# Sparse-attention block: queries with features on the partitions, stacked per head through DRAM

## The chip, the cores and the metric

One core of a Trainium2 chip runs the whole program: two layers of a hybrid block on 528 tokens (16 meta tokens and 512 of the sequence), all in f32. The metric is device time in microseconds, the median of three runs. The engines are TensorE (PE, with PEld for its weight loads), VectorE (DVE), ScalarE (ACT), GpSimd (POOL) and SyncE (SP), which here only issues DMAs.

## The reference

Each layer normalizes its input `h` (528 x 1024) and multiplies it by `w_in`. The columns are cut into attention queries, one key and one value head, a gate, the pooled branch with its gate, index queries and keys, and the merge gates. What matters here:

```
q = apply_rope(rms_norm(q.reshape(B, T, 8, 64), qn_g), cos_h, sin_h)
k = apply_rope(rms_norm(k, kn_g), cos, sin)
q_idx = apply_rope(q_idx.reshape(B, T, 8, 64), cos_h, sin_h)
k_idx = apply_rope(k_idx, cos, sin)
# per block of 128 queries
s = einsum('bqhd,bkd->bqhk', q_idx, k_idx)
score = einsum('bqhk,bqh->bqk', relu(s), w_idx * idx_scale)   # masked by chunk
_, sel = top_k(score, 128)
p = softmax(einsum('bqhd,bqkd->bqhk', q, k[sel]) * 0.125)     # valid ones
out = einsum('bqhk,bqkd->bqhd', p, v[sel])
```

`apply_rope` takes the 64 features of a head as two halves of 32 and returns `x * cos + (-second, first) * sin`. The attention output, gated, goes through `w_a`; the pooled branch (moving means over 2, 4, 8, 16 tokens, minus the input, times `pool_w`, gated) through `w_b`; both are weighed by sigmoid gates, summed and multiplied by `w_out`, and added to the input.

## The kernel before

The normalized input stands in SBUF with features on the partitions, split into `hhi` and `hlo` (the number rounded to f32r, and the rest), so that a product is three f32r products: `hhi` and `hlo` with a weight's high part, `hhi` with its low part. Weights come in chunks of 256 columns (1 MB, in two halves on SP's queue; four `raw` buffers, so two chunks) and are split in the same way into `w` tiles, eight of them, one chunk ahead of use. Three ways of splitting exist: ACT casts the high part and DVE subtracts (`high`, `low`, L185 and L189); for the chunks in `by_dma`, ACT writes minus the weight, rounded, and a POOL DMA adds the weight onto it (`minus`, L199), then ACT casts the high part; and a mixed one for the gates.

PE and DVE run in the order in which the program is written; the scheduler orders ACT, POOL and SP. `group_done` (L331) marks the end of a group of matmuls. It runs what `later(fn, n)` put off by `n` groups, one step of weight preparation, and steps of `fill` (score products or attention, `rate` of them a group). It then lets the selection (`sel`, the 16 rounds of max and replace on DVE) advance by a credit: the priced PE time less the priced DVE time since the last group.

A query group is `tok_group` (L481): 24 matmuls with 128 tokens of `hhi` or `hlo` as the stationary operand and 256 weight columns (four heads) moving, so that queries come out with tokens on the partitions. `q_post` (L585) then makes the rope with two DVE products and a POOL sum, splits into high and low (ACT, DVE), puts both side by side in `qs`, and four PE transposes a group turn that into 128 rows (64 high, 64 low features) by head by token; ACT evicts them to `qi` or `qq`. For the normed queries it also takes squares, sums and `rsqrt` (by POOL's `pow`) into `RQ`, used as a scale in the softmax; the gain sits in the tables `Cg` and `Sg`, which POOL makes (`tables`, L434). The 16 meta tokens are a group of their own in layer 0.

The order within a layer is: keys and values of the first half, index queries of the first half (group g=0), keys and values of the second half, index queries (second half, then all four blocks of g=1); the pool gate (`silb`, two chunks); the pooled product (two chunks of `u`, POOL's running sums `us`, DVE's `finish`, PE's `mix`); `queries(0)`; the attention gate (`sila`); `queries(1)`; then `w_b` and the merge gates (`mix_gates`), with attention as `fill`, and `w_a`, `w_out`. Scores of a block are made `FI` = 6 groups after its index queries (`index_steps`, L627). `attention` calls `ensure(i)` ahead of block `i`: it runs what is left of the selection that the block needs, all at once.

Of the kernel before, what the change touches and what calls it, by code (L numbers as in the profile page):

```python
# [29 lines left out]
PB = 4  # L30
R_ATT = (1.95, 1.7)
# [7 lines left out]
FI = 6  # L39
# [3 lines left out]
QI = 3  # L43
# [45 lines left out]
def tile_block(ctx: ExitStack, tc: tile.TileContext, x, meta, w_in, pool_w, w_a, w_b, w_out, rows, hgain, c_tab, out):  # L89
# [23 lines left out]
    mixed, by_dma, plain = set(), set(), set()  # L113
    for l in range(2):
        wi = w_rows(w_in[l], 0, w_in.shape[2])

        chunks.append([(wi[:, :, 2176:2432], 0)])
# [3 lines left out]
        order = [2432, 1664, 1920, 1408, 1152, 0, 640, 896, 256]  # L121
        chunks += [[(wi[:, :, c:c + 256], 0)] for c in order]
        chunks += [[(w_rows(w_b[l], c, 512), 0)] for c in (0, 512)]
        by_dma |= set(range(len(chunks) - 10, len(chunks)))
# [38 lines left out]
    def w_prep_enqueue(casts_first=False, after=None):  # L163
# [14 lines left out]
        def split(which):  # L178
            t = w_tile().rearrange("p (k e) -> p k e", e=cols)
            parts[which].extend(t[:, k] for k in range(kt // 2))  # L180
            return t

        his = {}

        def high(s):  # L185
            his[s] = split(0)
            act.copy(his[s], raws[c][s])

        def low(s):  # L189
            dve.tensor_sub(split(1), raws[c][s], f(his[s]))  # L190
            if s == 1:
                del raws[c]
                w_load()
# [194 lines left out]
    gains = one.tile([128, 2, 2, 64], F32, name="gains")  # L388
# [3 lines left out]
    dma(gains, bass.AP(tensor=hgain.tensor, offset=hgain.offset, ap=[[0, 128], [128, 2], [64, 2], [1, 64]]))  # L392
# [27 lines left out]
    Cg = one.tile([128, 5, 64], F32, name="Cg")  # L420
    Sg = one.tile([128, 5, 64], F32, name="Sg")
    BV = one.tile([128, 4, 2, 64], F32, name="BV")
    RQ = one.tile([128, 4, NH], F32, name="RQ")
    NR = one.tile([128, 4, NH], F32, name="NR")
# [4 lines left out]
    def sheet(n, name):  # L429
        if n > HB:  # L430
            return tmp.tile([128, 544], F32, tag="L", name=name, bufs=LB)
        return tmp.tile([128, HB], F32, tag="tt", name=name, bufs=6)

    def tables(l, keys):  # L434
        if keys:
            gk = tmp.tile([128, 64], F32, tag="gk", name="gk", bufs=1)
            gp.tensor_scalar(gk, gains[:, 1, l], -0.125, None, op0=OP.mult)
        g = gk if keys else gains[:, 0, l]

        def bc(g):  # L440
            return g[:, None, :].to_broadcast([128, 5, 64])

        def sw(g):
            return g.rearrange("p (a d) -> p a d", a=2)[:, None, ::-1, :].to_broadcast([128, 5, 2, 32])

        s4 = stab.rearrange("p t (a d) -> p t a d", a=2)
        gp.tensor_tensor(Cg, ctab, bc(g), op=OP.mult)
        gp.tensor_tensor(Sg.rearrange("p t (a d) -> p t a d", a=2), s4, sw(g), op=OP.mult)
# [32 lines left out]
    def tok_group(t, w):  # L481
        e = 256
        s, m = TOK[t]
        ps = bank("d")
        for h in H:
            for k in range(KT):
                pe.matmul(ps[:m, :e], h[:, k, s:s + m], w[0][k][:, :e], start=k == 0 and h is hhi, stop=False)
                if h is hlo and k == 3:
                    half_done()
        for k in range(KT):  # L490
            pe.matmul(ps[:m, :e], hhi[:, k, s:s + m], w[1][k][:, :e], start=False, stop=k == KT - 1)
        return ps

# [23 lines left out]
    def dense(w, mt_, a, n, rhs=H, kt=KT, late=False):  # L517
        ps = bank("d")
        c = slice(mt_ * 128, (mt_ + 1) * 128)
# [4 lines left out]
        for e, (ww, r, k) in enumerate(steps):  # L524
            pe.matmul(ps[:, :n], ww[k][:, c], r[:, k, a:a + n], start=e == 0, stop=e == len(steps) - 1)
# [4 lines left out]
    def swapped(ap, h):  # L530
        return ap.rearrange("p (h a d) -> p h a d", h=h, a=2)[:, :, ::-1, :]

    def kv_post(l, t, ps):
        s, m = TOK[t]
        p2 = ps[:m, :256].rearrange("p (g c) -> p g c", g=2)[:, :, 0:64]
        sq = tmp.tile([128, 64], F32, tag="tt", name="sq", bufs=6)
# [4 lines left out]
        t1 = tmp.tile([128, HB], F32, tag="tt", name="t1", bufs=6)  # L541
        t2 = tmp.tile([128, HB], F32, tag="tt", name="t2", bufs=6)
# [475 lines left out]
    for l in range(2):  # L1018
# [152 lines left out]
        def attend():  # L1171
# [8 lines left out]
            if l == 0:  # L1180
                yield from meta_attn(qm)
# [190 lines left out]
```

## Time and profile before

| | |
|---|---|
| runs | 760.87, 763.03, 762.77 us; median 762.77 |
| profiled execution | 762.81 us, its span 761.0 us |
| granted TensorE clock | 1.0 throughout |
| busy | PE 747.4, DVE 555.5, ACT 471.4, POOL 213.6 us |
| DMA | 96.94 MB, mean 127 GB/s |

The span is the time from the first to the last instruction of the profiled execution; all shares are of it. Busy times overlap between engines, and PE's are modelled ends of pipelined matmuls, so that PE's real pace is read from where the next one starts. L numbers are lines of the kernel; every PE and DVE instruction goes through one recording helper and has its line, L61, so one goes by tile names: `d<-w,hhi` is a query group with tokens stationary, `d<-hhi,w` one with the weights stationary.

### The profile page before, as it was taken

What the parts mean: (1) busy time and instruction counts of PE and PEld (TensorE: products, weight loads), DVE (VectorE), ACT (ScalarE), POOL (GpSimd) and SP (SyncE); (2) the same over time, 40 slices, a digit from 0 to 9 for tenths busy, and PEclk for the clock granted to TensorE, in tenths of its full rate; (3) what the DMA queues carried; (4) which work ended last, traced back from release to release, by engine and by line L of the source; (5) the groups of instructions that cost most, each with busy time, mean ns of one, the idle gap of its engine ahead of it and who ended that gap; (6) DMA issues with size and microseconds to landing.
All of it is one profiled execution on the core that took longest, in us unless ns stands there. A gap on an engine that the chain in (4) does not pass through costs nothing.

```text
span 761.0 us, 15628 instructions
## 1 busy us (share of the span) xinstructions
PE 747.4 (98%) x5911; PEld 713.8 (94%) x5911; DVE 555.5 (73%) x1412; ACT 471.4 (62%) x1044; POOL 213.6 (28%) x282
## 2 busy tenths in 40 slices
PE   8999999999999999999999999999999999999998
PEld 7899999999999999999998989988889899999998
DVE  5766886888888775894357668877899888678531
ACT  6668835638788795543245796455577788864320
POOL 2551164333011000062246410751411111005200
PEclk9999999999999999999999999999999999999999
DMA  7666784775031112543422687678811221136411
GB/s 258 206 158 168 168 205 115 157 205 141 7 106 57 57 57 89 192 140 112 140 85 84 166 177 171 170 153 204 207 44 56 87 82 56 57 124 212 138 43 42
DMA packets 73547, 96.94 MB, mean 127 GB/s; under 512 B 3664, under 2 KB 58736, under 8 KB 73472
## 3 DMA queue, kind: packets, MB, share of 16 engines
q1 hardware_dynamic: 67632, 74.89, 30.6%
q0 software_dynamic: 5760, 20.97, 15.2%
q8 instruction: 46, 0.75, 0.4%
q14 instruction: 29, 0.24, 0.1%
q10 hardware_dynamic: 80, 0.08, 0.0%
HBM read 66.41 MB, written 8.55 MB: 98 GB/s over the span
## 4 chain that ended last, share of the span: by engine, by line
PE 80%; DVE 11%; ACT 7%; issue 1%; POOL 0%; DVEq 0%; POOLq 0%; ACTq 0%
PE d L61 66%; PE a L61 10%; PE v L61 4%; DVE w L61 3%; ACT lt L713 2%; ACT w L233 1%; ACT lt L724 1%; DVE t L61 1%; DVE raw L61 1%; DVE nf L61 1%; ACT pt L740 1%; DVE lt L61 1%; DVE c L61 1%; DVE alo L61 1%; DVE s L61 1%
## 5 line engine op out<-in xcount | busy, mean ns | idle before, releaser
L61 PE MATMUL d<-hhi,w 128*128 128x256 f32 (+3 forms) x1408 | 287.1, 296 | 1.0 <-ACT hhi L1231 0.7
L61 PEld LDWEIGHTS d<-hhi,w 128*128 128x128 f32 x1408 | 225.5, 188 | 6.9 <-ACT hhi L1231 1.0
L61 PE MATMUL d<-hlo,w 128*128 128x256 f32 (+3 forms) x704 | 192.5, 294 | 0.0
L61 PEld LDWEIGHTS d<-hlo,w 128*128 128x128 f32 x704 | 132.1, 188 | 2.5 <-issue 0.2
L61 PE MATMUL d<-w,hhi 128*128 128x256 f32 (+1 forms) x800 | 124.2, 286 | 0.7 <-DVE w L61 0.5
L61 PEld LDWEIGHTS d<-w,hhi 128*128 128x128 f32 (+1 forms) x800 | 106.8, 185 | 3.8 <-issue 1.2
L61 DVE TENSOR_TENSOR w<-raw,w 128x512 fp32r<-128x512 f32 (+1 forms) x128 | 107.7, 851 | 2.4 <-ACT w L233 2.3
L61 PE MATMUL d<-hsum,w 128*128 128x264 f32 (+1 forms) x576 | 77.0, 286 | 0.1
L725 POOL TENSOR_SCALAR pm<-lt,rs 128x16 f32<-128x16 f32 x48 | 27.3, 583 | 173.8 <-DVE rs L61 166.8
L61 PE MATMUL d<-w,hlo 128*128 128x256 f32 (+1 forms) x400 | 73.4, 281 | 0.0
L61 PEld LDWEIGHTS d<-hsum,w 128*128 128x128 f32 x576 | 71.8, 188 | 1.1 <-ACT lt L724 0.3
L202 POOL DMA_DIRECT2D w<-raw x40 | 36.8, 934 | 104.7 <-ACT w L201 82.7
L233 ACT CAST w<-raw 128x512 fp32r<-128x512 f32 x96 | 56.8, 624 | 3.6 <-DVE raw L61 3.5
L61 PEld LDWEIGHTS d<-w,hlo 128*128 128x128 f32 (+1 forms) x400 | 58.0, 184 | 0.4
L1233 POOL TENSOR_TENSOR hlo<-ta,hhi 128x256 fp32r<-128x256 f32 (+1 forms) x28 | 28.2, 1018 | 96.5 <-PE d L61 83.2
L61 DVE MATCH_REPLACE8 sc<-m,sc 128x400 f32<-128x400 f32 (+2 forms) x100 | 54.3, 547 | 0.0
L61 DVE MAX8 m<-sc 128x8 f32<-128x400 f32 (+2 forms) x100 | 52.6, 556 | 0.8
L713 ACT ACTIVATE lt<-lt,mn,NR 128x144 f32<-128x144 f32 (+3 forms) x64 | 42.4, 665 | 16.3 <-DVE mn L61 16.3
L61 PE MATMUL d<-mhi,w 128*128 128x272 f32 (+2 forms) x192 | 47.7, 328 | 0.0
L201 ACT ACTIVATE w<-raw 128x1024 fp32r<-128x1024 f32 x40 | 41.3, 1057 | 10.1 <-PE d L61 10.1
L61 DVE SCALAR_TENSOR_TENSOR sc<-r,wsg,sc 128x144 f32<-128x144 f32 (+3 forms) x56 | 32.4, 581 | 16.3 <-ACT r L637 14.1
L602 POOL TENSOR_TENSOR t<-t,t 128x256 f32<-128x256 f32 (+1 forms) x34 | 31.1, 915 | 39.4 <-DVE t L61 39.4
(198 smaller groups left out, 1393.9 us busy)
## 6 DMA issues: line engine op xcount, KB each, us to landing
raw<-in_w_in_dram SPq DMA_DIRECT2D x72, 512.0 KB, 3.7
w<-raw POOLq DMA_DIRECT2D x40, 512.0 KB, 5.6
raw<-in_w_out_dram SPq DMA_DIRECT2D x16, 512.0 KB, 3.4
kept<-res SPq DMA_DIRECT2D x16, 264.0 KB, 2.9
res<-kept SPq DMA_DIRECT2D x16, 264.0 KB, 5.7
raw<-in_w_branch_b_dram SPq DMA_DIRECT2D x8, 512.0 KB, 4.5
raw<-in_w_branch_a_dram SPq DMA_DIRECT2D x8, 512.0 KB, 3.6
xt<-in_x_dram SPq DMA_DIRECT2D x4, 512.0 KB, 6.3
```

What stands on the lines that cost most here:

```text
L61: return fn(*a, **k)
L201: act.activation(t, raws[c][s], AF.Copy, scale=-1.0)
L202: gp.dma_start(t, raws[c][s], accum_op=OP.add)
L233: act.copy(t[:, 0], blk[src[n]])
L602: gp.tensor_tensor(t1[:m, :256], t1[:m, :256], t2[:m, :256], op=OP.add)
L713: act.activation(L[hh][:, :n], L[hh][:, :n], AF.Exp, scale=NR[:, i, h:h + 1], bias=mn[:, hh:hh + 1], accum_out=sm[:, hh:hh + 1])
L724: act.activation(L[hh][:, 16:n], L[hh][:, 16:n], AF.Copy, scale=rs[:, hh:hh + 1])
L725: (gp if j < 3 else dve).tensor_scalar(pms[i][:, 2 * j + hh, :], L[hh][:, 0:16], rs[:, hh:hh + 1], None, op0=OP.mult)
L740: act.copy(pt[:, :2 * len(bs)], tp[:, :256 * len(bs)].rearrange("p (a c) -> p a c", c=128))
L1233: pool_end = gp.tensor_sub(hlo[:, j, a:a + n], d, f(hhi[:, j, a:a + n]))
```

## The change

Query products exchange their operands: weights are stationary and tokens move (`dense` with `turn=True`), so queries come out with features on the partitions. For that the four query chunks of a layer (`turned`) are stored so that 128 columns are the first halves of four heads, and 128 the second halves; they are split by ACT and DVE, no longer with a DMA. `query_pair` makes two such groups for half of the tokens (256, or 272 with the meta tokens in layer 0). The rope is one DVE product per group with the turned tables `CS` (cosine and sine side by side) and two POOL sums; the result is split in place, and eight DMAs on SP write it to a DRAM tile `via`, from which two POOL DMAs (three with meta tokens) read it back as 128 rows by head by token. Squared norms are summed over partitions by small matmuls with `heads4`. `tok_group`, `q_post`, `tables` and the transposes go; `turned_tables` makes `CS` once, on PE, in the first layer.

`FI` becomes 8. `queries(0)` moves ahead of the pooled product and `queries(1)` ahead of the attention gate, with their weight chunks; index queries go by halves of the tokens. Buffers: `ks` moves to the `L` tiles, `tt` has five buffers for six, `P` tiles are 544 wide. Keys multiply their gain first.

```diff
+TB = 5
...
-FI = 6
+FI = 8
...
-QI = 3
...
+        turned |= {len(chunks) + i for i in (0, 2, 5, 8)}
...
-        order = [2432, 1664, 1920, 1408, 1152, 0, 640, 896, 256]
+        order = [2432, 1664, 1920, 0, 1408, 1152, 256, 640, 896]
...
-        by_dma |= set(range(len(chunks) - 10, len(chunks)))
+        by_dma |= set(range(len(chunks) - 10, len(chunks))) - turned
...
+            t = w_tile()
+            if c in turned:
+                parts[which].extend(t.rearrange("p (a k e) -> p k a e", a=2, k=4)[:, k] for k in range(4))
+                return t.rearrange("p (a h d) -> p a h d", a=2, d=32)
...
+        def raw_of(s):
+            return raws[c][s].rearrange("p k (h a d) -> p a (k h) d", a=2, d=32) if c in turned else raws[c][s]
...
+    def ptile(name, dt=F32):
+        return tmp.tile([128, 544], dt, tag="P", name=name, bufs=PB)
+    def turned_tables():
+        dve.tensor_tensor(heads4, hmask[:, ::2], hmask[:, 1::2], op=OP.add)
+        for h in range(4):
+            gp.memset(alt[32 * h:32 * h + 32], 2.0 * (h % 2) - 1.0)
+        for c, tab in enumerate((ctab, stab)):
+            for ts_ in ((0, 1, 2), (3, 4)):
+                tp = bank("a")
+                a = TOK[ts_[0]][0]
+                for t in ts_:
+                    s, m = TOK[t]
+                    for o in (0, 64):
+                        pe.matmul(tp[o:o + 64, s - a:s - a + m], tab[:m, t], ident[:m, :m], start=True, stop=True)
+                e = s + m
+                act.activation(CS[:, c, a:e], tp[:, :e - a], AF.Copy, scale=alt if c else 1.0)
...
-    def tok_group(t, w):
...
+        def part(wk):
+            if turn:
+                return wk[:, mt_]
+            return wk[:, mt_ * 128:(mt_ + 1) * 128]
...
+        kg = t2[:m, 128:256].rearrange("p (g d) -> p g d", g=2)
+        act.copy(kg[:, 1], p2[:, 1])
+        dve.tensor_tensor(kg[:, 0], p2[:, 0], gains[:m, l], op=OP.mult)
+        dve.tensor_tensor(t2[:m, :128].rearrange("p (g a d) -> p g a d", g=2, a=2),
+                          kg.rearrange("p g (a d) -> p g a d", a=2)[:, :, ::-1, :],
+                          stab[:m, t].rearrange("p (a d) -> p a d", a=2)[:, None].to_broadcast([m, 2, 2, 32]), op=OP.mult)
+        dve.tensor_tensor(v1, kg, ctab[:m, t, None, :].to_broadcast([m, 2, 64]), op=OP.mult)
...
-    def q_post(t, ps, normed, dst, g=0):
...
+
+
+    fetched = [None]
+
+    def query_pair(l, g, hf, w, normed, dst, between=None):
+        a, n = (HB, T - HB) if hf else (0, HB) if normed and l == 0 else (16, HB - 16)
+        M, sq = [None, None], [None, None]
+        via = dram.tile([128, 4, n], F32, name=f"via{l}{g}{hf}{int(normed)}")
+        rows_of = via.rearrange("(s a d) h t -> s h d a t", s=2, a=2)
+
+        def first(b, ps):
+            M[b] = ptile("turned", F32R)[:, :2 * n].rearrange("p (c n) -> p c n", c=2)
+            m = f(M[b])
+            p2 = ps[:, None, :n].to_broadcast([128, 2, n])
+            if normed:
+                dve.scalar_tensor_tensor(m, p2, gq[:, l, b:b + 1], CS[:, :, a:a + n], op0=OP.mult, op1=OP.mult)
+                sq[b] = tmp.tile([128, HB], F32, tag="tt", name="sq", bufs=TB)[:, :n]
+                act.activation(sq[b], ps[:, :n], AF.Square, scale=HD ** -0.5)
+            else:
+                dve.tensor_tensor(m, p2, CS[:, :, a:a + n], op=OP.mult)
+            if b:
+                v = f(M[0])
+                with tc.issue_after(fetched[0]) if fetched[0] else nullcontext():
+                    gp.tensor_tensor(v[:, 0], v[:, 0], m[:, 1], op=OP.subtract)
+                    gp.tensor_tensor(v[:, 1], v[:, 1], m[:, 0], op=OP.add)
+
+
+        def write(s):
+            for h in range(4):
+                dma(rows_of[s, h], f(M[1 - s][32 * h:32 * h + 32]))
 
         def second():
-            if normed and t == 0:
-                dve.tensor_tensor(v1, v1, rq[:m, :, None].to_broadcast([m, 4, 64]), op=OP.mult)
-            act.copy(qs[:m, :, 0:64], v1)
+            act.copy(M[1], f(M[0]))
+            write(0)
+            if normed:
+                dve.tensor_add(sq[0], sq[0], sq[1])
 
         def third():
-            dve.tensor_sub(qs[:m, :, 64:128], v1, f(qs[:m, :, 0:64]))
-
-        def trans():
-            tp = bank("a", F32R)
-            for h in range(4):
-                pe.transpose(tp[:, h * 128:h * 128 + m], qs[:m, h, :], identr[:m, :m])
-            act.copy(dst, f(tp).rearrange("p (h c) -> p h c", h=4)[:, :, :m])
-        later(second, 1)
-        later(third, QN if normed else QI)
-        later(trans, QN + 1 if normed else QI + 1)
+    fetched = [None]
+    def query_pair(l, g, hf, w, normed, dst, between=None):
+        a, n = (HB, T - HB) if hf else (0, HB) if normed and l == 0 else (16, HB - 16)
+        M, sq = [None, None], [None, None]
+        via = dram.tile([128, 4, n], F32, name=f"via{l}{g}{hf}{int(normed)}")
+        rows_of = via.rearrange("(s a d) h t -> s h d a t", s=2, a=2)
+        def first(b, ps):
+            M[b] = ptile("turned", F32R)[:, :2 * n].rearrange("p (c n) -> p c n", c=2)
+            m = f(M[b])
+            p2 = ps[:, None, :n].to_broadcast([128, 2, n])
+            if normed:
+                dve.scalar_tensor_tensor(m, p2, gq[:, l, b:b + 1], CS[:, :, a:a + n], op0=OP.mult, op1=OP.mult)
+                sq[b] = tmp.tile([128, HB], F32, tag="tt", name="sq", bufs=TB)[:, :n]
+                act.activation(sq[b], ps[:, :n], AF.Square, scale=HD ** -0.5)
+            else:
+                dve.tensor_tensor(m, p2, CS[:, :, a:a + n], op=OP.mult)
+            if b:
+                v = f(M[0])
+                with tc.issue_after(fetched[0]) if fetched[0] else nullcontext():
+                    gp.tensor_tensor(v[:, 0], v[:, 0], m[:, 1], op=OP.subtract)
+                    gp.tensor_tensor(v[:, 1], v[:, 1], m[:, 0], op=OP.add)
+        def write(s):
+            for h in range(4):
+                dma(rows_of[s, h], f(M[1 - s][32 * h:32 * h + 32]))
         def second():
-            if normed and t == 0:
-                dve.tensor_tensor(v1, v1, rq[:m, :, None].to_broadcast([m, 4, 64]), op=OP.mult)
-            act.copy(qs[:m, :, 0:64], v1)
+            act.copy(M[1], f(M[0]))
+            write(0)
+            if normed:
+                dve.tensor_add(sq[0], sq[0], sq[1])
         def third():
-            dve.tensor_sub(qs[:m, :, 64:128], v1, f(qs[:m, :, 0:64]))
-
-        def trans():
-            tp = bank("a", F32R)
-            for h in range(4):
-                pe.transpose(tp[:, h * 128:h * 128 + m], qs[:m, h, :], identr[:m, :m])
-            act.copy(dst, f(tp).rearrange("p (h c) -> p h c", h=4)[:, :, :m])
-        later(second, 1)
-        later(third, QN if normed else QI)
-        later(trans, QN + 1 if normed else QI + 1)
+            dve.tensor_sub(M[0], f(M[0]), f(M[1]))
+            write(1)
+            if normed:
+                norms()
+        def norms():
+            sp = bank("a")
+            for x_ in range(2):
+                o = TOK[1 + 2 * hf + x_][0] - a
+                pe.matmul(sp[:, 4 * x_:4 * x_ + 4], sq[0][:, o:o + 128], heads4, start=True, stop=True)
+            r = RQ[:, 2 * hf:2 * hf + 2, 4 * g:4 * g + 4]
+            dve.tensor_scalar(r, sp[:, :8].rearrange("p (t h) -> p t h", t=2), EPS, None, op0=OP.add)
+            gp.tensor_tensor(r, r, mhalf[:, :, None].to_broadcast([128, 2, 4]), op=OP.pow)
+            if a == 0:
+                qm2 = tmp.tile([128, 4, 16], F32, tag="qm2", name="qm2", bufs=1)
+                dve.tensor_tensor(qm2, heads4[:, :, None].to_broadcast([128, 4, 16]),
+                                  sq[0][:, None, 0:16].to_broadcast([128, 4, 16]), op=OP.mult)
+                def meta_norms():
+                    sp = bank("a")
+                    o = slice(64 * g, 64 * g + 64)
+                    pe.matmul(sp[o, 0:1], qm2.rearrange("p h c -> p (h c)"), ones, start=True, stop=True)
+                    dve.tensor_scalar(rqm[o], sp[o, 0:1], EPS, None, op0=OP.add)
+                later(meta_norms, 1)
+        def fourth():
+            todo = [(dst[x_], TOK[1 + 2 * hf + x_][0] - a, 128) for x_ in range(2)]
+            if a == 0:
+                todo.append((qm[:, 4 * g:4 * g + 4], 0, 16))
+            for d, o, m in todo:
+                fetched[0] = gp.dma_start(d, via[:, :, o:o + m]).ins
+        for b in range(2):
+            ps = dense(w, b, a, n, turn=True)
+            later(lambda b=b, ps=ps: first(b, ps), 1)
+            if b:
+                for k, fn in enumerate((second, third, fourth)):
+                    later(fn, 2 + k)
+            if between:
+                between(b)
+            group_done()
...
-        def index_queries(t, g, w):
-            qi = tmp.tile([128, 4, 128], F32R, tag="B", name="qi", bufs=8)
-            ps = tok_group(t, w)
-            later(lambda: q_post(t, ps, False, qi), 1)
-            later(lambda: fill.append(index_steps(t - 1, g, qi)), FI)
+        def index_queries(hf, g, w, between=None):
+            qi = [tmp.tile([128, 4, 128], F32R, tag="B", name="qi", bufs=8) for _ in range(2)]
+            query_pair(l, g, hf, w, False, qi, between)
+            for x_ in range(2):
+                later(lambda x_=x_: fill.append(index_steps(2 * hf + x_, g, qi[x_])), FI - 1)
...
-        for what, t in (("q", 1), ("q", 2), ("k", 3), ("k", 4), ("q", 3), ("q", 4)):
-            if what == "k":
-                ps = plain_group(t, raws[kv])
-                later(lambda t=t, ps=ps: kv_post(l, t, ps), 1)
-            else:
-                index_queries(t, 0, w)
-                if (l, t) == (0, 1):
-                    halved = norm_half(0, 1, rstd, LAG1)
+        def second_half(b):
+            nonlocal halved
+            if (l, b) == (0, 0):
+                halved = norm_half(0, 1, rstd, LAG1)
+                turned_tables()
+        index_queries(0, 0, w, second_half)
+        for t in (3, 4):
+            ps = plain_group(t, raws[kv])
+            later(lambda t=t, ps=ps: kv_post(l, t, ps), 1)
             group_done()
-            if (what, t) == ("k", 4):
-                del raws[kv]
-                w_load()
-                w_prep_enqueue(True, None if l else halved)
+        del raws[kv]
+        w_load()
+        w_prep_enqueue(True, None if l else halved)
+        index_queries(1, 0, w)
...
-        for t in range(1, 5):
-            index_queries(t, 1, w)
-            for k in (2 * t - 2, 2 * t - 1):
+        def keep(t):
+            for k in (2 * t, 2 * t + 1):
                 dma(kept[:, k, :], RES[0][:, k, :])
-            group_done()
+        for hf in range(2):
+            index_queries(hf, 1, w, lambda b, hf=hf: keep(2 * hf + b))
...
-            for t in range(0 if l == 0 else 1, 5):
-                if t == 0:
-                    dst = qm[:, 4 * g:4 * g + 4, :]
-                else:
-                    dst = QS[t - 1, g] = tmp.tile([128, 4, 128], F32R, tag="B", name="qq", bufs=8)
-                ps = tok_group(t, w)
-                later(lambda t=t, ps=ps, dst=dst: q_post(t, ps, True, dst, g), 1)
-                group_done()
-        tables(l, False)
+            for hf in range(2):
+                dst = [tmp.tile([128, 4, 128], F32R, tag="B", name="qq", bufs=8) for _ in range(2)]
+                QS[2 * hf, g], QS[2 * hf + 1, g] = dst
+                query_pair(l, g, hf, w, True, dst)
...
         sb = one.tile([128, 4, T], F32, tag="D", name="silb")
...
+        queries(0)
...
-        queries(0)
+        queries(1)
         sa = one.tile([128, 4, T], F32, tag="D", name="sila")
...
-        queries(1)
...
```

121 lines of the change are left out of this document (37 added, 84 removed).

## The prediction

> **What bounds the kernel now.** I read the page first: the busy line of each engine, and the chain that ended last by engine.
>
> ```profile
> PE 747.4 (98%) x5911; PEld 713.8 (94%) x5911; DVE 555.5 (73%) x1412; ACT 471.4 (62%) x1044; POOL 213.6 (28%) x282
> ...
> PE 80%; DVE 11%; ACT 7%; issue 1%; POOL 0%; DVEq 0%; POOLq 0%; ACTq 0%
> ```
>
> PE is busy for 747.4 of 761.0 us, and the chain runs through it for 80% of the span. That is an average, so the second view is a table of stretches, cut by hand along layer 0: score queries from 60, pooled product from 90, the two query chunks from 118 and 158, attention from 180. After the stretch come its length and then each engine's busy time and (in brackets) count, in the order PE, PEld, DVE, ACT, POOL, then granted clock, DMA share and GB/s.
>
> ```profile
> 60.00:90.00 30.00, 30.00 (x246) 30.00 (x245) 21.99 (x49) 24.44 (x52) 3.24 (x4) 1.00 0.73 177
> 90.00:118.00 28.00, 28.00 (x226) 27.47 (x226) 24.04 (x68) 16.20 (x27) 16.63 (x23) 1.00 0.72 167
> 118.00:138.00 20.00, 20.00 (x164) 19.23 (x162) 14.01 (x39) 11.37 (x24) 11.60 (x14) 1.00 0.56 125
> 158.00:180.00 22.00, 22.00 (x188) 21.29 (x187) 17.45 (x55) 13.49 (x26) 12.49 (x14) 1.00 0.73 170
> 180.00:240.00 60.00, 60.00 (x518) 59.37 (x517) 52.42 (x154) 49.31 (x135) 7.21 (x16) 1.00 0.24 71
> 240.00:300.00 60.00, 58.30 (x525) 55.74 (x526) 44.18 (x118) 46.11 (x108) 5.29 (x8) 1.00 0.21 63
> ```
>
> Where queries are made (118 to 138, 158 to 180) PE has no gap and every other engine has room: there the time is the count of PE instructions, at a clock of 1.00 throughout, and whatever leaves PE leaves the span. Attention is different: from 240 on PE loses 1.7 us in 60, and DVE has been full just before (52.42 of 60). A delay put on DVE there can reach PE.
>
> **What leaves PE.** Third view: PE's timeline. Its columns are start, length, engine, line, operation and tiles; the pitch of a group is the distance from its start to the next row's start, because lengths overlap.
>
> ```profile
> 39.59 0.46 PE L61 MATMUL a<-identr,qs 128*128 128x128 f32 x4
> 39.89 1.18 PE L61 MATMUL d<-w,hhi 128*128 128x256 f32 x8
> ...
> 116.88 1.28 PE L61 MATMUL d<-w,hhi 128*16 128x256 f32 x8
> ...
> 119.89 1.05 PE L61 MATMUL a<-us,pw 128*128 128x272 f32 x4
> ...
> 95.06 0.28 PE L61 MATMUL d<-hlo,w 128*128 128x256 f32 x1
> ...
> 97.91 0.29 PE L61 MATMUL d<-hlo,w 128*128 128x272 f32 x1
> ...
> 100.90 0.29 PE L61 MATMUL d<-hlo,w 128*128 128x256 f32 x1
> ```
> ```profile
> L61 PE MATMUL a<-identr,qs 128*128 128x128 f32 x128 | 14.7, 238 | 0.3 <-DVE qs L61 0.3
> L61 PE MATMUL d<-w,hhi 128*16 128x256 f32 x32 | 4.6, 285 | 0.0
> L61 PE MATMUL d<-w,hlo 128*16 128x256 f32 x16 | 2.2, 280 | 0.0
> L61 PE MATMUL a<-identr,qs 16*128 16x16 f32 x8 | 1.0, 223 | 0.0
> ```
>
> Queries come out of PE already turned, so the transposes go: 128 + 8 of them are 34 groups of four, and a group costs 39.89 - 39.59 = 0.30 us, 34 x 0.30 = 10.2 us. In layer 0 the 16 meta tokens had matmul groups of their own, at the full price of a group since the moving operand was the weight: 32 + 16 matmuls are two groups of 24. A group of 24 with 256 moving columns has a pitch of 97.91 - 95.06 = 2.85 us (the meta group at 116.88 took 3.01 beside other work), so 5.7 us go. Removed: **15.9 us**, all in stretches where PE was full.
>
> **What PE gains.** The meta tokens become 16 more columns of the first half: a 272-column group has a pitch of 100.90 - 97.91 = 2.99, 0.14 more than 2.85, on four groups: 0.6 us. New are 20 matmuls that turn the rope tables onto the partitions, 64 rows of output each, and 18 tiny ones (one or four columns) for the squared norms. The nearest rows are the attention's value products (64 rows of output, f32) and the sums of squares (one column), the first from the chain in order of time, the second from the timeline:
>
> ```profile
> 203.43 2.11 PE v L61 x24
> ...
> 381.02 0.38 PE L61 MATMUL a<-ones,sqs 128*128 128x1 f32 x2
> 381.26 0.36 PE L61 MATMUL a<-ones,tl 128*128 128x1 f32 x2
> ```
>
> 20 x 2.11 / 24 = 1.8 us; two tiny ones start 0.24 apart, 18 x 0.12 = 2.2 us. Added: 0.6 + 1.8 + 2.2 = 4.6 us; the same 96 big matmuls a chunk stay, with their operands exchanged. Net on PE: 4.6 - 15.9 = **-11.3 us**. Bounds: if the tiny and turning matmuls cost half, -13.3; twice, -7.3.
>
> **What DVE, ACT and POOL get.** Costs from the groups by shape:
>
> ```profile
> L61 DVE TENSOR_TENSOR t<-d,consts 128x256 f32<-128x256 f32 x32 | 12.1, 415 | 4.8 <-PE d L61 4.2 <-POOL t L602 0.6
> L61 DVE TENSOR_TENSOR qs<-t,qs 128x256 fp32r<-128x256 f32 x32 | 13.3, 415 | 0.0
> L61 DVE TENSOR_TENSOR raw<-raw 128x512 f32<-128x512 f32 x32 | 22.0, 688 | 0.6
> L61 DVE TENSOR_TENSOR w<-raw,w 128x1024 fp32r<-128x1024 f32 x32 | 42.9, 1356 | 0.1
> L201 ACT ACTIVATE w<-raw 128x1024 fp32r<-128x1024 f32 x40 | 41.3, 1057 | 10.1 <-PE d L61 10.1
> L602 POOL TENSOR_TENSOR t<-t,t 128x256 f32<-128x256 f32 x32 | 29.7, 927 | 35.3 <-DVE t L61 35.3
> L454 POOL TENSOR_TENSOR RQ<-RQ,mhalf 128x4 f32<-128x4 f32 x16 | 18.7, 1169 | 5.0 <-DVE RQ L61 4.9
> L202 POOL DMA_DIRECT2D w<-raw x40 | 36.8, 934 | 104.7 <-ACT w L201 82.7
> ```
>
> DVE: two token blocks took 2 x 3 operations of 0.415 (2.5 us); a pair now takes two products and one subtraction of 512 columns, 3 x 0.688 = 2.1. That saves 0.4 for each of 16 pairs, 6.4, and on the normed ones about another 0.4 x 8; against it the two query chunks a layer leave the DMA-made split, and DVE makes their low parts, 4 chunks x 2 x 1.356 = 10.8. DVE stays level within 2 us. ACT loses the evictions of the transposes and 4 chunks x 2 of the 1.057 casts: lighter. I cost both at nothing: in the query stretches DVE has 6 and 4.5 us free, ACT 8 or more, and PE is what hides them. The key path now multiplies from SBUF copies with the same number of operations or one less: nothing.
>
> POOL keeps two sums a pair (2 x 0.927) and gets two reads back from DRAM (three where the meta tokens are in it). No row shows such a read. Between 0.934 (the same issue instruction, moving 512 KB in 128 rows) and 3.7 (four times that, since a read has four rows a partition). I take 1.7: nearer the row, whose time has a fixed part. It matters in one place: the pooled product now has two pairs' reads queued on POOL among its running sums. In 90 to 118 POOL was busy 16.63; four of its weight issues leave (3.7), one pair's two sums (1.9) and two powers (2.3) come: 17.1, and five reads of 1.7 make 25.6, with 28 there. It fits but is tight, since a read also waits for its writes with everything behind it on POOL: the sums, DVE's finishing step, PE's pooled product. I charge 1 us for both layers; bounds 0 and the rival below.
>
> **The trip through DRAM.** Each pair issues eight writes on SP, between weight loads.
>
> ```profile
> 23.40 4.82 SPq L1063 DMA_DIRECT2D kept<-res  x8
> ```
> ```profile
> w<-raw POOLq DMA_DIRECT2D x40, 512.0 KB, 5.6
> ...
> kept<-res SPq DMA_DIRECT2D x16, 264.0 KB, 2.9
> ```
>
> Eight writes are 4.8 us of issue, 2.9 to land; a read 1.7 and at most 5.6 to land: 15 us. The scores wait eight groups, and three of those lie between issuing the read and using it (about 3 x 3.5 us with score work between), so PE should not see it. At both ends of a layer's first pair (SP behind a weight load, POOL behind the reads, weight splits on POOL behind those) I charge 0.5 us in all; bounds 0 and 4.
>
> **What comes late next.** Scores two groups later means selection later on DVE, and its schedule is fixed when the program is written, by credits. In the order of the changed program, six selection instructions of each layer are left for the forced drain before the third attention block (before: none in layer 0, two in layer 1).
>
> ```profile
> 200.57 0.69 DVE L61 MATCH_REPLACE8 sc<-m,sc 128x528 f32<-128x528 f32 x1
> ...
> 223.93 0.57 DVE L61 CUSTOM_DVE_ANT_0 lt<-a,sc 128x400 f32<-128x400 f32 x1
> ```
> ```profile
> L61 DVE MATCH_REPLACE8 sc<-m,sc 128x400 f32<-128x400 f32 x32 | 17.8, 558 | 0.0
> ```
>
> Selection ended at 201.3 in layer 0, 22.7 us before that block's first use (223.93). Now six more, 3 x (0.558 + 0.69) = 3.7 us, stand in one piece on a full DVE, and behind them that block's logits and the evictions of the gates' PSUM banks. PE hides part: three banks are in flight, about 1.4 us each half group. Between 0 and 7.5 for both layers; I take 2.5.
>
> **The sum,** against the profiled execution's own 762.81 us (span 761.0, 1.8 around it; the median of the runs is 762.77, so no correction): -11.3 + 1 + 0.5 + 2.5 = -7.3, **755.5 us**.
>
> **Rivals.**
> *All of it lands* (0.15): lags cover everything; 762.8 - 11.3 = 751.5. For it: the full PE line, lighter ACT. Against: DVE full in attention.
> *The late selection costs its whole price* (0.12): -11.3 + 7.5 + 1.5 = -2.3, 760.5. For it: DVE at 52.42 of 60; against: it stood idle more after 240.
> *DVE delays the reads' issue* (0.05): a read whose four rows each find a 0.558 us selection instruction in the way takes 0.934 + 4 x 0.558 = 3.2. Five make 17.1 + 15.8 = 32.9 in 28 us, 4.9 over; four, in layer 1, 1.8 over: -11.3 + 6.7 + 0.5 + 2.5 = -1.6, 761.2. Against it stands the spread of the forty issues that there are (shortest, median, longest in ns), all beside a DVE that is busy 73% of the span:
>
> ```profile
> L202 POOL DMA_DIRECT2D w<-raw x40: 850/874/1288, 47.2 to 544.7; - x40
> ```
>
> [...]
>
> *POOL becomes the bound in the pooled product, slower* (0.16): a read at 3.7 and a 3 us wait for the writes at each of two pairs. Layer 0: 17.1 + 18.5 + 6 = 41.6 in 28 us, 13.6 over; layer 1, with four reads, 9.9 over. 762.8 - 11.3 + 23.5 = 775.0. It decides once both overruns together pass 11.3, which with those waits is at 2.3 us a read. For it: POOL works in order, and its sums are what DVE and then PE wait for; against: the row just shown.
>
> *It does not do what it says*: if the turned weights gave slower matmuls, the pitch would exceed 2.85; both operands are still 128 columns wide and contiguous in SBUF, so I give it nothing apart from the cases.
>
> **How the numbers follow.** 0.52 for the forecast (751 to 760), 0.15 + 0.12 + 0.05 + 0.16 for the rivals. A difference of 0.3%, 2.3 us, is about what a measurement here can tell from none. Faster: 0.52 + 0.15 + half of the late selection + 0.01 = 0.74; same: the other half and 0.04 of the delayed reads = 0.10; slower 0.16. Range: from 750.5, just under the full saving, to 765, into the slower case, leaving out its upper part.
>
> **What would show it.** Right: no 'identr,qs' rows; PE's count of 256-column groups at 2.85 pitch; PE without gaps from 60 to 180 minus about 7 us of length in layer 0 up to the attention; reads on POOL between 0.9 and 2.5 us; a PE gap after the third block's drain of 1 to 2 us a layer. Wrong: reads on POOL over 2.5 us with PE waiting on DVE 'us' or 'silb'; PE waiting for 'qi' (the trip longer than the lag) or for 'w' in the first gate chunk; waits of PE for 'mn' of over 3 us at the third block.

## The result, and the profile after

The changed kernel takes 773.69 us (median of 4 runs, 773.42 to 776.81), against 762.02 us before: **1.6% slower**, ratio 1.0163 with an interval of 1.0132 to 1.0194. The prediction was 755.5 us. The profiled execution took 773.77 us, its span 771.9.

The page of the changed kernel: busy time and instructions, the chain that ended last, and two of the DMA queues (q1 holds what SP issues, q0 what POOL issues).

```profile
PE 740.4 (96%) x5803; PEld 705.5 (91%) x5803; DVE 564.4 (73%) x1341; ACT 446.8 (58%) x996; POOL 223.3 (29%) x292
...
q1 hardware_dynamic: 78448, 83.29, 34.8%
q0 software_dynamic: 22560, 25.24, 18.0%
...
PE 58%; DVE 23%; ACT 8%; issue 4%; DMA 3%; POOL 2%; SPq 1%; DVEq 0%; ACTq 0%; POOLq 0%
```

PE has less to do and less of the chain: 58% where it had 80%, and DVE has twice its share. Before, q1 had 67,632 packets and q0 5,760; now they have 27,600 more. What PE waited for, in microseconds, times and the longest, first after and then before:

```profile
PE a L61 <- ACT lt L773: 6.7, 4, 4.3
PE a L61 <- DVE us L61: 3.9, 2, 2.1
PE d L61 <- DVE w L61: 3.0, 3, 1.8
PE d L61 <- ACT zb L1246: 2.7, 1, 2.7
...
PE a L61 <- ACT r L686: 2.2, 3, 1.4
```
```profile
PE d L61 <- DVE t L61: 1.4, 2, 0.8
PE a L61 <- ACT lt L724: 1.4, 3, 0.9
```

Waits of up to 4.3 us stand where, past the start, none was over 1 us. To compare kernels I took from each trace the start of the last matmul; the sum, over neighbouring matmuls, of the distance between their starts beyond the usual pitch of that shape, where this excess is over 0.3 us (stalls); and half of the time, up to the last matmul, at a granted clock of 0.5 (clock). The rest is PE's work.

| kernel | last matmul | stalls | clock | rest |
|---|---|---|---|---|
| before | 757.4 | 14.0 | 0.0 | 743.4 |
| after | 767.8 | 31.6 | 3.4 | 732.8 |
| small_trip | 754.7 | 20.6 | 3.4 | 730.7 |
| no_drain | 759.1 | 24.3 | 1.7 | 733.1 |
| sp_reads | 758.5 | 22.5 | 3.4 | 732.6 |
| no_trip_no_drain | 748.0 | 15.4 | 0.0 | 732.6 |
| far_act | 752.2 | 18.0 | 1.7 | 732.5 |

PE's work fell by 10.6 us, as forecast (11.3). Stalls grew by 17.6, and 3.4 went to the clock. There are three places.

**The second layer's queries and merge gates.** The same stretch after, before and in small_trip (below), with PE's busy time first behind the length, and the DMA share last but one:

```profile
420.00:450.00 30.00, 26.74 (x171) 23.71 (x170) 14.54 (x22) 15.74 (x28) 12.05 (x16) 1.00 1.05 241
```
```profile
420.00:450.00 30.00, 29.69 (x217) 27.50 (x216) 20.27 (x41) 24.86 (x51) 9.31 (x10) 1.00 0.75 185
```
```profile
420.00:450.00 30.00, 29.88 (x188) 27.11 (x189) 17.95 (x31) 24.38 (x46) 10.34 (x15) 1.00 0.83 201
```

PE is idle for 3.3 of 30 us, and the DMA share is 1.05: the times of all packets add up to as much as 16 engines have in the stretch. ACT's timeline shows who passes that on: it stands behind a weight load here, and behind a fetch in the merge gates, and what PE needs is queued behind it on ACT (`r`, then `zb`).

```profile
447.44 1.05 ACT L196 CAST w<-raw 128x1024 fp32r<-128x1024 f32 x1 [5.66 <-DMA raw<-in_w_in_dram]
...
555.31 1.30 ACT L924 CAST hhi<-hsheet 128x512 fp32r<-128x512 f32 x2 [7.25 <-DMA hsheet<-far]
```

**The pooled product.** POOL's timeline in the first layer: it stands 4.54 us for the writes of `via`, then makes the reads and the power, and only at 117.10 the first running sum; DVE's `finish` and PE's `mix` come after that.

```profile
113.11 1.59 POOL L662 DMA_DIRECT2D qq<-via  x2 [4.54 <-DMA via<-turned]
114.69 0.74 POOL L662 DMA_DIRECT2D qm<-via  x1
115.45 1.68 POOL L644 TENSOR_TENSOR RQ<-RQ,mhalf 128x8 f32<-128x8 f32 x1
117.10 1.09 POOL L1196 TENSOR_TENSOR us<-u 128x543 f32<-128x543 f32 x1
```

**The forced selection in attention.** DVE's timeline before the third block of the second layer (its ends and one round between), PE's next row, and two stretches of the clock:

```profile
602.18 1.18 DVE L61 MAX8 m<-sc 128x8 f32<-128x400 f32 x2
603.28 0.07 DVE L61 MATCH_VALUE_LOAD sc<-m,sc 128x8 f32 x1
603.34 0.56 DVE L61 MATCH_REPLACE8 sc<-m,sc 128x400 f32<-128x400 f32 x1
...
606.80 0.70 DVE L61 TENSOR_SCALAR sc<-sc 128x400 f32<-128x400 f32 x2
```
```profile
608.30 1.09 PE L61 MATMUL a<-consts,lt 128*128 128x128 f32 x3 [4.30 <-ACT lt L773]
```
```profile
598.00:607.30 9.30, 6.00 (x49) 5.79 (x47) 9.08 (x22) 4.18 (x12) 0.00 (x0) 1.00 0.20 58
607.30:614.10 6.80, 5.79 (x24) 5.57 (x25) 6.04 (x19) 5.72 (x14) 0.13 (x1) 0.50 0.10 23
```

DVE selects for 5.3 us in one piece, PE stands 4.3 us, and the granted clock is 0.50 for 6.8 us from 1.0 us before the stall ends, which costs up to 3.4 more. In the first layer the same block is preceded by 4.2 us of selection, and PE stands 1.9 us.

### The profile page after: what moved, and what is told of

Read it like the earlier page. It is cut to its first block, busy times and chain, and to the rows that moved or that the text cites. A ratio compares the mean times of both kernels' runs of the same rounds, so it can differ in the third digit from the quotient of the medians.

```text
span 771.9 us, 15595 instructions
## 1 busy us (share of the span) xinstructions
PE 740.4 (96%) x5803; PEld 705.5 (91%) x5803; DVE 564.4 (73%) x1341; ACT 446.8 (58%) x996; POOL 223.3 (29%) x292
## 4 chain that ended last, share of the span: by engine, by line
PE 58%; DVE 23%; ACT 8%; issue 4%; DMA 3%; POOL 2%; SPq 1%; DVEq 0%; ACTq 0%; POOLq 0%
PE d L61 48%; PE a L61 7%; DVE w L61 5%; DVE sc L61 4%; PE v L61 4%; DVE m L61 2%; ACT lt L762 2%; DMA hsheet<-far 2%; ACT w L242 1%; DVE turned L61 1%; ACT lt L773 1%; POOL us L1196 1%; DVE raw L61 1%; DVE nf L61 1%; DMA via<-turned 1%
## 5 line engine op out<-in xcount | busy, mean ns | idle before, releaser
L61 PE MATMUL d<-hhi,w 128*128 128x256 f32 (+3 forms) x1920 | 386.5, 294 | 3.7 <-DVE w L61 2.7
L61 PEld LDWEIGHTS d<-hhi,w 128*128 128x128 f32 x1920 | 306.1, 188 | 11.7 <-DVE w L61 3.6
L61 PE MATMUL d<-hlo,w 128*128 128x256 f32 (+3 forms) x960 | 255.2, 291 | 0.0
L61 PEld LDWEIGHTS d<-hlo,w 128*128 128x128 f32 x960 | 180.3, 188 | 3.4 <-issue 1.0
L196 ACT CAST w<-raw 128x1024 fp32r<-128x1024 f32 x40 | 42.0, 1049 | 17.1 <-PE d L61 9.6
L61 PE MATMUL d<-w,hhi 128*128 128x256 f32 x256 | 46.8, 287 | 0.0
L61 PEld LDWEIGHTS d<-w,hhi 128*128 128x128 f32 x256 | 38.7, 189 | 0.0
L773 ACT ACTIVATE lt<-lt,rs 128x128 f32<-128x128 f32 (+3 forms) x64 | 32.7, 559 | 9.8 <-DVE rs L61 9.7
L61 PEld LDWEIGHTS d<-mhi,w 128*128 128x128 f32 x192 | 32.7, 189 | 5.8 <-ACT zb L1246 3.1
L686 ACT ACTIVATE r<-a,wab 128x272 f32<-128x272 f32 (+2 forms) x80 | 34.6, 488 | 5.4 <-PE a L61 5.3
```

Of the source, the lines that this page charges most:

```text
L61: return fn(*a, **k)
L196: act.copy(his[s], raw_of(s))
L686: act.activation(r[:, n - 1::-1] if i == 0 else r[:, o:o + e], ps[:, :e], AF.Relu, scale=wab[:, i, h:h + 1])
L773: act.activation(L[hh][:, 16:n], L[hh][:, 16:n], AF.Copy, scale=rs[:, hh:hh + 1])
```

## The experiments

Ratios are to the kernel before, on the same chip. The medians of the kernel before lie between 760.99 and 762.02 us in these comparisons, so a difference between two runs can be off by about 1 us.

**no_trip** replaces the writes by nothing and the reads by copies:

```diff
-                dma(rows_of[s, h], f(M[1 - s][32 * h:32 * h + 32]))
-                fetched[0] = gp.dma_start(d, via[:, :, o:o + m]).ins
+                src = M[1] if o < 128 else M[0]
+                act.copy(d, f(src).rearrange("p c n -> p (c n)")[:, :4 * m].rearrange("p (h t) -> p h t", h=4))
```


> Leaves out the trip through DRAM: no writes to via and no reads back; ACT copies the split query tiles straight into qi, qq and qm, so that the values there are not the queries (the scores are of other numbers). Everything else stays. Theory A (the trip is what cost: 14 MB more on DMA engines that were already 0.6 to 0.9 busy, and POOL waiting for writes): the PE stalls at 121 (2.2 us, DVE us), 421 (2.0, DVE w), 447 (2.2, ACT r), 498 (2.2, DVE us) and 554 (2.8, ACT behind hsheet<-far) go, 11.4 us, so about 762. Theory B (the late selection and what it does in attention is most of it): only the query stages gain, 2 to 4 us, so 770 to 772.

759.69 us, 0.9985 (0.9976 to 0.9994): theory A, and 2 us more. Without the trip the kernel is 14 us faster; that includes what POOL and ACT no longer wait for.

**no_drain** is `FULL = 1.1`.

> One constant: the credit of the selection is 1.1 times the priced PE time, in place of 1.0; when the program is written, nothing of the selection is then left for the forced drain before the third attention block (10 to 12 instructions a layer were). Theory B (the drain is what cost in attention: stalls of 2.1 us at 220 and 4.5 us at 604, and the lower granted clock of 0.83 behind the second): 765 to 768, with a clock of 1.0 throughout. Rival (DVE is full, the work only moves ahead, and stalls come earlier): 772 to 774.

764.52 us (runs from 760.65 to 765.94), 1.0029 (1.0012 to 1.0046): theory B holds as well. `lt` is no longer among the longest waits of PE, and where the drain was PE is full, at full clock:

```profile
590.00:610.00 20.00, 19.93 (x178) 19.25 (x177) 17.16 (x50) 17.73 (x45) 2.92 (x6) 1.00 0.32 83
```

**sp_reads** and **order_back**: reads by `nc.sync.dma_start(f(d), ...)`, with the `issue_after` of the next sums gone; and the two query chunks moved back.

> The reads back from via are issued on SP in place of POOL, so POOL no longer waits for writes, and the waits stand on SP ahead of weight loads. Theory A1 (POOL's order is the cost): stalls at 121 and 498 go, 4.4 us: 769. Theory A2 (the traffic is the cost, not who waits): 772 to 775; if weight loads fall behind the waiting reads, more, with PE waiting for DVE w.

764.55 us, 1.005 (1.0032 to 1.0069): 9 us, twice what A1 gave. Not only the waits for `us` went, those for `r` too, though DMA moves the same bytes. The kernel is 3.9 us ahead there, so this is the same work as in 420 to 450 above, and ACT's cast behind the same weight load:

```profile
416.00:446.00 30.00, 29.04 (x187) 26.10 (x186) 17.14 (x28) 19.77 (x36) 9.86 (x10) 1.00 1.02 254
```
```profile
442.19 1.05 ACT L196 CAST w<-raw 128x1024 fp32r<-128x1024 f32 x1 [0.97 <-DMA raw<-in_w_in_dram]
```

The DMA share is 1.02, nearly that of the changed kernel, and PE is idle for 1.0 us in place of 3.3; ACT stands 0.97 us in place of 5.66. So a share of 1 alone does not stop PE: what counts here is whether the load that ACT stands for is late. SP's rows show a difference that may be the reason, changed kernel first:

```profile
439.27 1.08 SPq L144 DMA_DIRECT2D raw<-in_w_in_dram  x2
440.48 9.10 SPq L623 DMA_DIRECT2D via<-turned  x8
```
```profile
437.64 1.57 SPq L144 DMA_DIRECT2D raw<-in_w_in_dram  x2
440.85 1.20 SPq L661 DMA_DIRECT2D qi<-via  x2
442.10 3.93 SPq L622 DMA_DIRECT2D via<-turned  x8
```

Where SP has to wait for a pair's writes before it issues the reads, the next eight writes start 4.5 us behind the load, and not 1.2. No run changes this alone.

> The changed kernel with queries(0) again behind the pooled product and queries(1) behind the attention gate, their weight chunks with them. Theory A1 (POOL's order in the pooled product: sums stand behind reads that wait for writes): the stalls at 121 and 498 go, 4.4 us, and the end of layer 1's queries stays: 769. Theory B (DMA traffic as such, or the late selection): the same traffic in other places, 772 to 775. A third one, that the old order makes attention wait for qq: 775 or more with PE waiting for qq.

781.44 us (runs from 775.15 to 784.87; the trace is of the shortest), 1.0282 (1.0258 to 1.0306): the third case. PE waits for `qq` (1.8 us) and far more for the drain (10.2 us for `lt`, 6.7 in the changed kernel).

**sp_no_drain**, both edits; **sp_no_drain_hs**, the cast of the sheet a group later; **no_trip_no_drain**; and **before_no_drain**, the kernel before with `FULL = 1.1`.

> Both edits at once: reads issued on SP, and the selection's credit at 1.1. If POOL's order and the drain are two causes, the gains add: 773.7 - 9.2 - 9.2 = 755, with no PE gap over 1.5 us but the one behind hsheet<-far at 545. Rival: they take away the same slack (each alone already ended at 764.5), and it stays at 760 to 764.

760.16 us, 0.9985 (0.9976 to 0.9994): the rival, at its lower edge: the two gains overlap. The gap behind `hsheet` at 546 grew to 3.9 us, with 6.8 us of half clock.

> As sp_no_drain, and ACT's cast of the sheet fetched back (hsheet<-far) one group later in the w_b stage of both layers. If the PE gap of 2.8 us in the second layer's w_b stage comes from ACT standing 8.1 us behind that DMA, the gap goes and with it the lower granted clock behind it (0.95 and 0.88 over 20 us): 2 to 4 us less than sp_no_drain. Rival: the wait moves to a later user (the s1 product waiting for the last sheet): the same or more.

759.09 us, 0.9972 (0.996 to 0.9984), against 0.9985: the intervals overlap, and the gap is still 2.8 us. It settles nothing.

> As no_trip (no writes to via and no reads back, ACT copies in their place, so the queries' values are not the right ones), with the credit at 1.1. The sum of the prediction without its charges, 762.8 - 11.3 = 751.5, is what this must show if PE's work really fell by 11.3 us: 759.7 - 2.1 - 4.5 of gaps and 2 to 3 of lower clock = 750 to 752. Rival (the work on PE fell by less): 755 or more with no gap left.

753.7 us, 0.9901 (0.9887 to 0.9915), between the two, 2 us over the expectation. Its table row has the same work as the changed kernel (732.6), stalls nearly as before, and no clock lost: the saving is there once trip and drain are gone.

> The kernel before with the credit at 1.1 alone. If the drain became a cost only through the change (before, nothing in the first layer and four instructions in the second were forced), no difference: 761 within 1. Rival (the credit was too small all along, and the gain has nothing to do with the change): 757 or less.

763.61 us, 1.0031 (1.002 to 1.0042): neither, a loss of 2.6. The higher credit gains nothing in the old order, so the drain is a cost of the change.

**no_wait**: the reads take their data from the weights, so POOL waits for no write.

```diff
+                src = bass.AP(tensor=w_in.tensor, offset=w_in.offset, ap=[[w_in.shape[2], 128], [256, 4], [1, m]])
+                with tc.issue_after(summed[0]):
+                    fetched[0] = gp.dma_start(d, src).ins
```


> The changed kernel, with the reads still on POOL, as many and with the same pieces of 512 B, but from a region of the weights in DRAM, so that none waits for the writes to via; the writes stay. The values in qi, qq and qm are then not the queries. If what cost was POOL's wait for the writes with its sums and weight splits behind it: like sp_reads, 764 to 766. If it was POOL's own time for the reads: still 772. If it was the traffic: 772.

772.71 us, 1.0141 (1.0123 to 1.016). PE's waits for `us` are gone, but its longest for `r` grew from 1.4 to 3.7 us: ACT stands 8.0 us for the weight load, and transfers land later (KB each, us to landing; 3.9, 5.4 and 5.6 in the changed kernel):

```profile
via<-turned SPq DMA_DIRECT2D x112, 64.0 KB, 5.7
...
qi<-in_w_in_dram POOLq DMA_DIRECT2D x16, 256.0 KB, 7.9
qq<-in_w_in_dram POOLq DMA_DIRECT2D x16, 256.0 KB, 9.8
```

So POOL's wait explains the pooled product's stalls. For the rest the run is unclear, since it changed the landing too; POOL not waiting is not enough to bring what sp_reads gained.

**far_act** (sp_no_drain, with `act.dma_start` for `hsheet`), and on it **far_act_fi6** (`FI = 6`); **sp_order_back** (sp_reads with the old order).

> As sp_no_drain (reads on SP, credit 1.1), with the sheets of the merge gates (hsheet<-far) fetched on ACT's own queue in place of SP's. If they are late because they stand behind 1 to 1.5 MB of weight loads in SP's queue: landing 4 to 5 us in place of 8, the PE gap of 3.9 us in the second layer's w_b stage and the lower clock behind it go: 754 to 756. If they are late because all DMA engines are full there (share 1.06): no gain, 759 to 761.

757.35 us, 0.9948 (0.9931 to 0.9965): **0.5% under the kernel before**, a small difference, but clear of the interval. The gap at 546 is gone, but not as expected: the sheets of 256 KB still take 8.2 us to land (8.6 in sp_no_drain), those of 132 KB 7.1 (10.0), and ACT still stands 5.5 us for a sheet (7.2).

> As far_act, with FI = 6 again, so scores two groups earlier. If the trip needs the eight groups: PE waits for qi, several gaps of 1 us, 3 us or more worse than far_act. If eight is more than it needs: the same or 1 us better, since selection starts earlier.

765.07 us (runs from 760.83 to 771.9; the trace is of one with 771.13), 1.0062 (1.0032 to 1.0091): with six groups PE waits for the trip.

```profile
PE a L61 <- DMA qi<-via: 7.2, 2, 3.6
```

> Reads on SP as in sp_reads (764.6), and queries(0) and queries(1) back behind the pooled product and the attention gate. If the new order is what gives the trip its time: some 5 to 8 us worse, 770 to 772, with PE waiting for qq at the start of attention or selection drained for longer. If the old order was harmed only by POOL's waits: 764 to 766.

776.12 us, 1.0201 (1.0179 to 1.0223), 11.6 us over sp_reads: with the trip, the new order is worth that much. So moving the queries ahead was not the fault, nor were the eight groups one too many, as far_act_fi6 shows.

**two_write**: four writes a pair in place of eight.

```diff
-            for h in range(4):
-                dma(rows_of[s, h], f(M[1 - s][32 * h:32 * h + 32]))
+            for a_ in range(2):
+                dma(via.rearrange("(s a d) h t -> s a h d t", s=2, a=2)[s, a_], f(M[1 - s])[:, a_])
```


> The changed kernel with four DMAs of 128 KB a pair writing to via, by rows halves over all 128 partitions, in place of eight of 64 KB over 32 partitions; bytes and pieces (1 KB) are the same, reads stay on POOL. If weight loads are late because SP issues 16 writes in 13.3 us ahead of one (in the second layer, 425.9 to 439.3): the gaps at 421, 447 and 554 shrink, POOL waits less, so the ones at 121 and 498 too: 762 to 768. If they are late because the DMA engines are full: no change, 772 to 775.

840.4 us, 1.1048 (1.1015 to 1.108): neither. Two stretches in which almost only these writes were in flight show 0.26 and 0.29 of 16 engines:

```profile
461.50:463.90 2.40, 2.40 (x23) 2.40 (x22) 0.00 (x0) 2.40 (x5) 2.37 (x4) 1.00 0.26 77
450.50:454.00 3.50, 3.47 (x30) 3.26 (x29) 2.03 (x3) 0.00 (x0) 0.00 (x0) 1.00 0.29 99
```

Why the share is so low is not shown: the trace does not name the engines, and no run changes the shape of the writes alone. What it led to is: POOL stands 110.7 us for the writes, 40.8 in the changed kernel, and `w<-raw` lands in 8.1 us, 7.1 there.

**best_a, best_b, best_c** stand on the same four writes.

> far_act (reads on SP, credit 1.1, sheets fetched on ACT's queue) and the four writes. If SP's issue time is still a cost there: 754 to 756. If not: 757, as far_act.

> As best_a, with the small matmuls of the squared norms one group later than the operation that DVE makes for them. The PE gap of 2.3 us at 517 (PE waiting for DVE sq) goes, and with it the lower clock behind it where it comes: 2 to 3 us less than best_a. Rival: DVE is behind there whatever PE asks for, and the next user of DVE waits: the same.

> As best_b with the credit at 1.05: up to six instructions a layer are left for the drain, and DVE is less crowded in the query stages. If 1.1 hurts DVE in the query stages (as it made the kernel before 2.6 us slower): 1 to 2 us less than best_b. If the drain is what counts: a gap of 1 to 2 us before the third attention block of the second layer, 1 to 3 us more.

790.13 (1.0371), 787.12 (1.0331) and 783.64 us (1.0284): the writes spoil all three, and they say little else.

**small_trip** keeps every issue and its order, and sends one row of each:

```diff
-                dma(rows_of[s, h], f(M[1 - s][32 * h:32 * h + 32]))
+                dma(rows_of[s, h][:1], f(M[1 - s][32 * h:32 * h + 1]))
-                fetched[0] = gp.dma_start(d, via[:, :, o:o + m]).ins
...
+                fetched[0] = gp.dma_start(d[:1], via[:1, :, o:o + m]).ins
```


> The changed kernel with every DMA of the trip still issued, in nearly the same order on SP and POOL and with the same waits, but each carrying one row of its 32 or 128 (2 or 4 pieces); ACT copies the split queries into qi, qq and qm as in no_trip, so the values are not the queries. If the late loads come from the bytes (14 MB, 1536 pieces a pair on engines at shares of 0.9 to 1.2): the gaps at 447 and 554 go and most of no_trip's gain comes, 760 to 763. If they come from SP's and POOL's issue time and order: they stay, 770 to 774.

761.49 us, 0.9999 (0.9987 to 1.0011): **the bytes, not the issues**. With the bytes goes all that waits for them: POOL stood 40.8 us for the writes in the changed kernel, and 5.3 here. Its packets are near those of before, and of PE's waits only the drain and the small ones are left; `us`, `zb` and `r` are gone:

```profile
q1 hardware_dynamic: 68720, 75.09, 32.7%
q0 software_dynamic: 5696, 16.85, 12.0%
```
```profile
PE a L61 <- ACT lt L775: 6.7, 4, 4.3
PE d L61 <- POOL idle L389: 2.4, 1, 2.4
PE d L61 <- DVE w L61: 1.9, 2, 0.9
PE a L61 <- DVE lt L61: 1.3, 1, 1.3
```

**best_d**: far_act with the credit at 1.05 and the norms later.

> far_act (757.4), with the eight writes, the credit at 1.05 in place of 1.1 and the small matmuls of the squared norms one group later. If the gap of 2.3 us at 517 is PE asking too early for what DVE makes: it goes, 754 to 756. Rival (with the smaller credit four to six instructions of the second layer are left for the drain and PE waits there): 757 to 759.

757.41 us, 0.995 (0.9931 to 0.9968), the rival, and the same as far_act. The gap at 517 went, and one of 2.4 us at 545, where PE waits for `lt`, took its place.

## Why the prediction was wrong

- **What leaves PE and what it gains** (-11.3): right. The table gives -10.6, and no_trip_no_drain shows the same work.
- **DVE, ACT and POOL beside it** (nothing): DVE got 8.9 us more, not level within 2, mainly because the sum of a pair's two squares (`sq<-sq`) is missing from its list: six of the eight took 8.2 us. ACT got 24.6 less. PE's waits for split weights came to 3.0 us, the longest 1.8.
- **Reads on POOL** (1.7 us each, bounds 0.934 to 3.7): outside the bounds, below. The 32 reads took 0.79 and 0.83 us in the mean, the longest 1.17. With that falls the rival in which DVE delays them: that a selection instruction holds up a row of a read was the author's estimate, and no run shows it. The fixed part that the choice of 1.7 rested on is nearly all of an issue: 0.74 us for the two reads of 32 KB, 0.79 and 0.83 for those of 256 KB, 0.95 for the 512 KB of a weight.
- **The pooled product** (1 us): PE waited 3.9 us for `us`. The cause was in the text as a rival, POOL's wait for the writes; its price was the error. These waits went both in sp_reads and in no_wait.
- **The trip through DRAM** (0.5 us, bounds 0 and 4): *the main step that failed.* Its latency was about right: reads land in 5.4 to 5.6 us (5.6 forecast), writes in 3.9 (2.9), and no row has PE waiting for `qi` or `qq`. But a trip was costed as a delay that eight groups cover, and its bytes were costed at nothing, while the share of 0.73 in the very rows quoted left a quarter of the engines. Without the bytes the kernel is 12.2 us faster (small_trip, 773.69 - 761.49), 11.0 of it stalls. They fell on others: weight loads, fetches, and POOL's queue. Bytes are not a price by themselves: with SP issuing the reads, the same bytes leave the time 3.1 us over small_trip (764.55 - 761.49). The cost came from the bytes together with the order in which the changed kernel issued them.
- **Late selection** (2.5 us, bounds 0 and 7.5): the mechanism was right and the size wrong. In the second layer ten instructions, 5.3 us, were forced, not six of 3.7, and eight, 4.2 us, in the first (the kernel before had none and four, not none and two); PE hid about 1 us in the second. The waits for `lt` grew by 5.3 us, and up to 3.4 of half clock came on top: 8.7. no_drain gave back 9.2, of which 5.8 are waits for `lt`.
- **The clock**, taken as 1.00: it has no term in the sum, and the stall of 4.3 us was paid again in part: 6.8 us at 0.50, up to 3.4.
- **The slower rival** (775.0) came out near the time, by chance: of its 13.6 and 9.9 us in the pooled product, 3.9 were there, and its reads of 3.7 us took 0.8.

Charges of 4.0 against 17.6 of stalls and 3.4 of clock: that is nearly the whole miss of 18.2. The two large causes overlap a little: alone, no_trip gains 14.0 and no_drain 9.2, both together 20.0, and without both the changed order is 7.3 us faster than before (no_trip_no_drain). Open in part is why the same bytes cost 9.1 us less when SP issues the reads. 3.9 are the waits for `us`, and 2.2 the waits for `r`, whose weight load was late; but that SP's wait, by holding back the next writes, made it land earlier is argued from the rows and not shown by a run. Nor is it shown why the gap at 546 went when the sheets were fetched on ACT's queue.

## What to carry to other kernels

A detour through DRAM had two prices here, a delay (3.9 us in the median for a write to land, 5.4 and 5.6 for a read) and a load (12.2 us, small_trip): add its bytes and pieces to the DMA share of the stretch it falls in, and where that comes near 1, look for the engine that stands behind a late load with the bottleneck's work queued after it. The share alone does not decide: at 1.05 PE lost 3.3 us of 30 here, at 1.02, with the reads on another queue, 1.0. Whatever moves scores later moves the selection behind them too, so its budget has to be set anew with the order. Before making DMAs fewer and larger, measure the DMA share while they are in flight: four writes of 128 KB in place of eight of 64 KB ran at 0.26 to 0.29 here, and the kernel took 66.7 us more.

## What the runs showed of the hardware

In these runs a PE stall of 3.1 us or more cost more than its length. In the traces of the changed kernel and its variants (two_write and best_a to best_c left out), the lower clock is exactly 0.5, for 3.41 us or twice that, and begins between 3.2 us before and 1.8 us after the end of a stall. All 14 stalls of 3.1 us and over came with it, and 8 of the 20 between 1.9 and 2.9 us; once it followed two stalls of 1.6 and 1.3 us in a row. So a stall of 4 us would cost up to 1.7 or 3.4 us more, half of those lengths. Why a stall between 1.9 and 2.9 us was followed by the lower clock in some cases and not in others is not shown.

That two_write cost 66.7 us (840.4 - 773.69), by a change that halved the number of writes, was not expected either.
